# RWKV-7 time mixing on one core: each pair of heads with its r and v projections, low-rank products and chain together, beside a key projection of the next token group

## The chip, the core and the metric

The kernel runs on one NeuronCore of a Trainium2 chip. Its time is the device time of one launch in microseconds (us); the lower, the better. The engines are TensorE (PE, with its weight loads as PEld), VectorE (DVE), ScalarE (ACT), GpSimd (POOL) and SyncE (SP, which here issues nearly all DMAs). Each takes its instructions in a fixed order and waits on semaphores for what the others produce.

## The reference

One inference step of a two-layer hybrid decoder with D = 1024, on 1048 tokens: 16 learned tokens and 1024 prompt tokens in one sequence, and 8 decode tokens with states of their own. Layer 0 is a causal Conformer convolution, layer 1 is RWKV-7 time mixing with 16 heads of 64; after each comes a squared-ReLU MLP (1024 to 4096 to 1024). Layer 1 is what the change touches:

```python
xr, xw, xk, xv, xa, xg = (h + xx * x_mix[i] for i in range(6))   # xx = previous row - h
r, k, v = xr @ w_r, xk @ w_k, xv @ w_v
w_log = -softplus(-(w0 + tanh(xw @ w1) @ w2)) - 0.5
decay = exp(-exp(w_log))
a = sigmoid(a0 + (xa @ a1) @ a2)
g = sigmoid(xg @ g1) @ g2
kk = normalised per head (k * k_k)
k = k * (1 + (a - 1) * k_a)
S = S * decay + (S @ -kk) (kk * a) + v k      # step by step over the tokens, per head
y = S @ r
out = ((groupnorm(y) + bonus(r, k, v)) * g) @ w_o
```

## The kernel before

Everything lies feature by token: a tile has 128 features (one pair of heads, index p of 8) on the partitions and the tokens along the row. Layer 0 and its MLP run first and end at 1126 us of the trace. Then comes time mixing, which the change rewrites, then the output projection `w_o` and the second MLP.

**Token groups.** Time mixing takes the 1048 tokens in four groups `G1` of 272, 256, 256 and 264 (g = 0 to 3). For each, `prepare(g)` (line 773) loads the normalised rows `hx` and makes the differences `xx`; `mix` (line 808) makes one mixed input tile `mx` on DVE. `mixer_in(g)` (line 822) then has three stretches:

- eight r projections (lines 927 to 940; `proj`, line 848, is eight 128x128 weight blocks against eight `mx` tiles, 16 records in the trace), each copied out by ACT and written to DRAM (`d_rk`); then the narrow product for the gate (`narrow`, line 867, `p_g`), which reads `hx` directly;
- eight k projections (lines 951 to 966), written to `d_rk` too, each with the second gate product (`lora2`, `l_g`) and with its squares summed over heads by a matmul into `pn`; then the norms (`r16`) and the narrow product for decay and a (`p_wa`);
- eight v projections (lines 1043 to 1102), one for each pair of heads. With them goes the **chain** of that pair: `l_w` and `l_a` (second low-rank products), the spread of the norms (`pb`, line 1063), then on DVE and ACT the normalised key, the running sum of the log decay, two exponentials and the four scaled operands `ab` (lines 1064 to 1096), then in `finish` (line 984), one pair later, transposes of v (`vt`), small matmuls of 64 rows by 32 columns (`nn`, line 1015), the bonus (`pk`, line 1031), and DMAs to `d_ab`, `d_v`, `d_n` and `d_bv`. r and k come back from `d_rk` by `fetch` (line 1037).

**The recurrence.** Tokens are also cut into 17 chunks of up to 64 (`chunk`, line 1202). Chunk c needs the `ab` of all eight pairs of its group, and so runs beside the next group. Its `front` (line 1150) loads the operands, makes the products `A` and, once for four chunks, on DVE the `inverses` (line 1124) of 32x32 blocks (`tt`, `ni`: 60 instructions in a row that each need the one before). Then come the small matmuls `gg`, `po`, `W`, `U`, `S`, `Y` with DVE and ACT steps between them, which must follow one another. How far the recurrence goes beside the projections is set by `tick` (line 1420): each call adds `PACE[g]` to a credit, and chunks advance as far as the credit pays (`advance`, line 1318). In the v stretch `beside` gives half as much for a call (`VSLOW`) and steps `prepare` of the next group. What is left of the recurrence runs beside `w_o` and the MLP of the first output group (`until`), as do the decode tokens (`decode_step`) and the normalisation and gating of y (`norm_gate`).

**What sets the order.** The code states the dependences and a priority; the tile framework puts every engine's instructions into a fixed order when the kernel is built. Weight blocks (512 KB) go through `load_raw` (line 143) into a ring of six buffers, four projections ahead.

Of the kernel before, what the change touches and what calls it, by code (L numbers as in the profile page):

```python
# [8 lines left out]
F32 = mybir.dt.float32  # L9
# [3 lines left out]
ALU = mybir.AluOpType  # L13
# [35 lines left out]
def hybrid_step(tc, x_prompt, x_sample, state_conv, state_shift, state_wkv, meta_tokens,  # L49
# [10 lines left out]
    with ctx:  # L60
        def pool(stack, name, bufs, **kw):
            return stack.enter_context(tc.tile_pool(name=name, bufs=bufs, reuse_waits="tile", **kw))
# [14 lines left out]
        d_rk = dram.tile([P, KT, 2, T], F32, name="d_rk")  # L77
# [113 lines left out]
        def bank(name, tag="mm"):  # L191
            return cur[tag].tile([P, 512], F32, name=name, tag=tag)
# [577 lines left out]
        prep = {}  # L770
        VSLOW = 0.5

        def prepare(g):
# [34 lines left out]
            def mix(i, k):  # L808
# [8 lines left out]
        wrkv = col_stream([(w, p, f"w{s}{g}_{p}") for g in range(4)  # L817
                           for s, w in (("r", rwkv_w_r[0]), ("k", rwkv_w_k[0]), ("v", rwkv_w_v[0]))
                           for p in range(KT)], 4)
        carry = {"tail": lambda: None}  # L820

        def mixer_in(g, tick, ahead):
# [22 lines left out]
            def mixed(i):  # L845
                return [mix(i, k) for k in range(KT)]

            def proj(w, act, wid, name, fill=None):
                ps = bank(nm("p", name))
                for k in range(KT):  # L850
                    nc.tensor.matmul(ps[:wid, :n], w[:, k, :], act[k], start=k == 0, stop=k == KT - 1)  # L851
                    if fill and k in (2, 5):
                        fill()
                return ps
# [50 lines left out]
            def second(parts, name):  # L905

                raw = wide.tile([P, D], F32, name=nm(name) + "_raw", tag="wide")
                for rows, src in parts:
                    nc.sync.dma_start(raw[rows], src)
                return blocks_of(raw)  # L910

            dd = lambda p, i, src: nc.gpsimd.tensor_copy(ddec[:, p, i, :], src)
            allp = slice(0, P)

            def beside(gen, places, slow=1.0):

                calls = [0]

                def trace():
                    tick(slow)  # L920
                    if calls[0] % 3 in places:
                        next(gen, None)
                    calls[0] += 1
                return trace


            act = mixed(0)
            both = lambda: tick(1.0)
            for p in range(KT):
                both()  # L930
                ps = proj(next(wrkv), act, P, f"r{p}", both)
                if p == 0:
                    carry["tail"]()
                if p == KT - 2:
                    ws = narrow_w(1, "g")
                r = t_("st", p, "em", 2)
                nc.scalar.copy(r[:, :n], ps[:, :n])
                nc.sync.dma_start(d_rk[:, p, 1, c0:c0 + n], r[:, :n])
                if npr < n:
                    dd(p, 4, r[:, npr:n])  # L940


            gate(ws)
            act = mixed(2)
            pn = bank(nm("pn"), "x")
            wg2 = second([(allp, rwkv_g2[0])], "wg2")
            add_pn = lambda: None

            def to_pn(p, sq):
                return lambda: nc.tensor.matmul(pn[:, :n], head_sel(p), sq[:, :n], start=p == 0, stop=p == KT - 1)  # L950
            for p in range(KT):
                both()
                ps = proj(next(wrkv), act, P, f"k{p}", both)
                k_ = t_("st", p + KT, "em", 2)
                nc.scalar.copy(k_[:, :n], ps[:, :n])
                nc.sync.dma_start(d_rk[:, p, 0, c0:c0 + n], k_[:, :n])
                sq = t_("sq", p, "rk", 2)
                nc.scalar.activation(sq[:, :n], ps[:, :n], AF.Square, scale=vec("k_k", p))
                add_pn()
                add_pn = to_pn(p, sq)  # L960
                if p == KT - 2:
                    ws = narrow_w(0, "wa")
                ps = lora2(wg2, p, lg, f"g{p}")
                gt = t_("gt", p, "vv", 2)
                nc.scalar.copy(gt[:, :n], ps[:, :n])
                nc.sync.dma_start(d_g[:, p, c0:c0 + n], gt[:, :n])
            r16 = lorap.tile([P, N1], F32, name=nm("r16"), tag="lf")
            r16p = [lorap.tile([P, N1], F32R, name=nm("r16" + q), tag="r16" + q)[:, :n] for q in "hl"]

            def norms():  # L970
                add_pn()
                nc.vector.tensor_scalar(r16[:, :n], pn[:, :n], L2_EPS * L2_EPS, None, op0=ALU.max)
                nc.scalar.activation(r16[:, :n], r16[:, :n], AF.Sqrt)
                nc.vector.reciprocal(r16[:, :n], r16[:, :n])
                split(*r16p, r16[:, :n], nc.vector)

            norms()
            decay_rate(ws)


            act = mixed(3)
            both = beside(ahead, (1, 2), VSLOW)
# [54 lines left out]
            def fetch(p):  # L1037
                rk2 = pr.tile([P, 3, N1], F32, name=nm("rk2", p), tag="rk2", bufs=2)
                nc.sync.dma_start(rk2[:, 1:, :n], d_rk[:, p, :, c0:c0 + n])
                return rk2  # L1040

            late, later = (lambda: lambda: None), lambda: None
            for p, rk2 in ahead_of(fetch):
                both()
                if p == 0:
                    ps = proj(next(wrkv), act, P, f"v{p}", both)
                    wa2 = second([(HALF[0], rwkv_w2[0]), (HALF[1], rwkv_a2[0])], "wa2")
# [7 lines left out]
                if p:  # L1055
                    ps = proj(next(wrkv), act, P, f"v{p}", both)
# [5 lines left out]
                pb = bank(nm("pb", p), "x")  # L1062
# [39 lines left out]
                next(ahead, None)  # L1102
            for _ in ahead:
                pass
# [313 lines left out]
        PACE = [0, 1.7, 1.7, 0.98]  # L1418

        def tick(g, slow):  # L1420

            advance(PACE[g] * slow, NCH - 1)
            next(ng0, None)

        for g in range(4):
            if g == 0:
                for _ in prepare(0):
                    pass
            mixer_in(g, lambda slow=1.0: tick(g, slow), ranked(PP, prepare(g + 1)) if g < 3 else iter(()))
# [162 lines left out]
```

## Time and profile before

| what | value |
|---|---|
| time, median of 3 runs | 2861.14 us (2853.25 to 2863.94) |
| profiled execution, its own time | 2865.08 us |
| its span | 2863.4 us, mean granted TensorE clock 0.975 |
| time mixing, first r projection to the last v projection's pair | 1126.5 to 1845 us |
| PE busy over the span | 2756.3 us (96%) |
| DVE, ACT, POOL busy | 1795.2, 1185.9, 1436.1 us |
| DMA traffic | 428.15 MB, mean 150 GB/s |

How to read it. Each engine's busy time is the union of its instructions' records. A busy PE can still be slow in two ways that the share does not show: the granted clock (column PEclk, 1.00 is full) and small matmuls that follow one another more slowly than they could. In a row of the timeline the first number is the start, the second the length of the merged records; as matmuls overlap, the cost of a row is the distance from its start to the next row's start. "idle before" names what the engine waited for last.

### The profile page before, as it was taken

Reading aid. Unit: us, or ns where it says so; the run is one execution under the profiler, and the core shown is the slowest. Engines: PE = TensorE matmul, PEld = TensorE weight load, DVE = VectorE, ACT = ScalarE, POOL = GpSimd, SP = SyncE. Lnnn points to the kernel's source line nnn. Section 1 sums busy time; section 2 is a strip of 40 time slices with the busy share of each in tenths; the row PEclk is TensorE's granted clock in tenths of the full one; section 3 lists DMA queues with packets and bytes.
Section 4 is the critical chain, followed back from the end, with each engine's and each line's share of the span. In section 5 each row is a group of like instructions: output and inputs, shape, how many; then the busy total and the mean of one; then the engine's idle time right before and its main releaser. Section 6 shows DMA issues by size and latency. Waiting matters only on the chain.

```text
span 2863.4 us, 51601 instructions
## 1 busy us (share of the span) xinstructions
PE 2756.3 (96%) x19594; PEld 2553.4 (89%) x19594; DVE 1795.2 (63%) x3618; ACT 1185.9 (41%) x2230; POOL 1436.1 (50%) x1983
## 2 busy tenths in 40 slices
PE   8999999999999899979999999979999999999998
PEld 7999999999999898858778877768889999999998
DVE  5999999995465545167455771679756764443444
ACT  5545444543364332232434643534345552222223
POOL 6677877987788774000000110265448783333332
PEclk9999999999999999989999999989999999999999
DMA  6663544454445643778768785675557742222211
GB/s 177 176 186 88 154 139 133 134 178 140 140 129 149 192 140 120 214 198 197 199 181 217 212 215 150 195 179 149 131 152 215 208 134 86 67 74 67 67 60 41
DMA packets 659270, 428.15 MB, mean 150 GB/s; under 512 B 126840, under 2 KB 609208, under 8 KB 659022
## 3 DMA queue, kind: packets, MB, share of 16 engines
q1 hardware_dynamic: 652780, 421.93, 52.1%
q10 hardware_dynamic: 6018, 2.89, 0.4%
q8 instruction: 155, 2.54, 0.4%
q14 instruction: 93, 0.76, 0.1%
q0 software_dynamic: 224, 0.03, 0.0%
HBM read 353.03 MB, written 72.66 MB: 149 GB/s over the span
## 4 chain that ended last, share of the span: by engine, by line
PE 37%; DVE 7%; POOL 5%; DMA 3%; issue 3%; ACT 1%; SPq 0%; DVEq 0%; POOLq 0%; ACTq 0%
PE ps_in L187 3%; PE ps_in L188 3%; PE ps_in L189 3%; POOL wo_lo L162 3%; PE out L187 3%; PE out L189 3%; PE out L188 3%; PE p_v L851 3%; PE p_k L851 2%; POOL wi_lo L162 2%; PE p_r L851 2%; PE A L1176 2%; DVE ni L1136 1%; DVE tt L1135 1%; PE U L1260 1%
## 5 line engine op out<-in xcount | busy, mean ns | idle before, releaser
L162 POOL TENSOR_TENSOR wo_lo<-wo_raw,wo_hi 128x256 fp32r<-128x256 f32 x736 | 563.4, 799 | 286.3 <-ACT wo_hi L157 267.4
L162 POOL TENSOR_TENSOR wi_lo<-wi_raw,wi_hi 128x256 fp32r<-128x256 f32 x640 | 490.5, 799 | 272.0 <-ACT wi_hi L157 259.7
L187 PE MATMUL out<-hh,wo_hi 128*128 128x352 f32 (+2 forms) x1536 | 502.7, 327 | 18.5 <-DVE h L340 9.3
L187 PE MATMUL ps_in<-m_h,wi_hi 128*128 128x352 f32 (+2 forms) x1536 | 498.8, 325 | 12.3 <-ACT m_h L269 11.5
L340 DVE TENSOR_TENSOR h<-h,out 128x352 f32<-128x352 f32 (+2 forms) x768 | 385.5, 509 | 188.3 <-PE out L189 187.2
L189 PE MATMUL out<-hl,wo_hi 128*128 128x352 f32 (+2 forms) x1536 | 494.8, 325 | 6.8 <-DVE hl L141 6.8
L188 PE MATMUL out<-hh,wo_lo 128*128 128x352 f32 (+2 forms) x1536 | 497.7, 324 | 0.0
L189 PE MATMUL ps_in<-m_l,wi_hi 128*128 128x352 f32 (+2 forms) x1536 | 497.0, 324 | 0.0
L188 PE MATMUL ps_in<-m_h,wi_lo 128*128 128x352 f32 (+2 forms) x1536 | 496.7, 324 | 0.0
L504 DVE SCALAR_TENSOR_TENSOR cv<-u,wdw,cv 128x352 f32<-128x352 f32 (+2 forms) x720 | 376.5, 572 | 0.7
L157 ACT CAST wi_hi<-wi_raw 128x1024 fp32r<-128x1024 f32 x160 | 168.0, 1050 | 396.5 <-PE out L189 189.0
L157 ACT CAST wo_hi<-wo_raw 128x1024 fp32r<-128x1024 f32 x184 | 192.8, 1049 | 311.5 <-PE out L189 144.1
L187 PEld LDWEIGHTS out<-hh,wo_hi 128*128 128x128 f32 x1536 | 292.2, 190 | 26.3 <-DVE h L340 13.7
L187 PEld LDWEIGHTS ps_in<-m_h,wi_hi 128*128 128x128 f32 x1536 | 290.9, 189 | 15.6 <-ACT m_h L269 11.7
L189 PEld LDWEIGHTS out<-hl,wo_hi 128*128 128x128 f32 x1536 | 291.7, 191 | 9.0 <-DVE hl L141 8.1
L188 PEld LDWEIGHTS out<-hh,wo_lo 128*128 128x128 f32 x1536 | 292.2, 190 | 1.3
L188 PEld LDWEIGHTS ps_in<-m_h,wi_lo 128*128 128x128 f32 x1536 | 290.7, 189 | 1.7
L189 PEld LDWEIGHTS ps_in<-m_l,wi_hi 128*128 128x128 f32 x1536 | 290.6, 189 | 1.8
L327 DVE SCALAR_TENSOR_TENSOR r<-ps_in,rs_m 128x352 f32<-128x352 f32 (+2 forms) x192 | 98.5, 515 | 235.7 <-PE ps_in L189 232.0
L141 DVE TENSOR_TENSOR hl<-s,hh 128x352 fp32r<-128x352 f32 (+2 forms) x192 | 143.8, 750 | 112.0 <-ACT hh L140 111.9
L329 ACT ACTIVATE s<-r 128x352 f32<-128x352 f32 (+2 forms) x192 | 93.7, 490 | 141.6 <-DVE r L327 141.3
L851 PE MATMUL p_r<-mx,wr_raw 128*128 128x256 f32 (+2 forms) x512 | 123.4, 396 | 4.1 <-DVE n L1017 4.1
(350 smaller groups left out, 4926.9 us busy)
## 6 DMA issues: line engine op xcount, KB each, us to landing
wi_raw<-in_w_mlp_in_dram SPq DMA_DIRECT2D x160, 512.0 KB, 4.0
wo_raw<-in_w_mlp_out_dram SPq DMA_DIRECT2D x160, 512.0 KB, 3.7
wr_raw<-in_rwkv_w_r_dram SPq DMA_DIRECT2D x32, 512.0 KB, 6.0
wk_raw<-in_rwkv_w_k_dram SPq DMA_DIRECT2D x32, 512.0 KB, 4.2
wv_raw<-in_rwkv_w_v_dram SPq DMA_DIRECT2D x32, 512.0 KB, 4.5
d_ab<-ab SPq DMA_DIRECT2D x32, 512.0 KB, 4.0
pg_raw<-in_conv_w_pw_dram SPq DMA_DIRECT2D x24, 512.0 KB, 4.6
pa_raw<-in_conv_w_pw_dram SPq DMA_DIRECT2D x24, 512.0 KB, 4.7
```

The source lines that it names most:

```text
L141: eng_lo.tensor_sub(lo, src, hi.bitcast(F32))
L157: nc.scalar.copy(hi[:, :a * b], raw[:, :a * b])
L162: eng_lo.tensor_sub(lo[:, cs], raw[:, cs], hi[:, cs].bitcast(F32))
L187: nc.tensor.matmul(ps, w[0], act[0], start=first, stop=False)
L188: nc.tensor.matmul(ps, w[1], act[0], start=False, stop=False)
L189: nc.tensor.matmul(ps, w[0], act[1], start=False, stop=last)
L327: nc.vector.scalar_tensor_tensor(r[:, :n], ps[:, :n], 0.0, rs[:, :n], op0=ALU.max, op1=ALU.mult)
L329: nc.scalar.activation(s[:, :n], r[:, :n], AF.Square)
L340: nc.vector.tensor_add(hv[:, 4 * i + m, :], hv[:, 4 * i + m, :], ps[:, :n])
L504: nc.vector.scalar_tensor_tensor(acc[m][:, :n], ug[:, m, j:j + n], wdw[:, m, j:j + 1], acc[m][:, :n], op0=ALU.mult, op1=ALU.add)
L851: nc.tensor.matmul(ps[:wid, :n], w[:, k, :], act[k], start=k == 0, stop=k == KT - 1)
L1176: nc.tensor.matmul(ps[:, i * 2 * P:(i + 1) * 2 * P], bk[:, j + i, :], xa[:, j + i].rearrange("p q x -> p (q x)"), start=True, stop=True)
```

## The change

- The order of time mixing. The key projections, with their squares, are taken out of `mixer_in` into a generator `keys(g)`. Those of group 0 run ahead of everything; those of group g+1 run one by one beside the pairs of group g. `mixer_in(g)` starts with both narrow products (gate, then decay and a), and then has one loop over the eight pairs: r projection, `l_g`, `l_w`, `l_a`, v projection, the chain, `finish` of the pair before, and one key projection of the next group.
- r no longer goes to DRAM and back: it is copied straight into the pair's tile `rk2`. `d_rk` (r and k) becomes `d_k`.
- `g2`, `w2`/`a2`, the second low-rank weights, are loaded once and kept, not once for each group.
- The gate's sigmoid is written with Tanh (0.5 tanh(x/2) + 0.5).
- Buffers: weight ring 6 to 5, narrow weights 4 to 2, mixed inputs 20 to 25; `st`, `gt` get tags of their own, and `r16h`/`r16l` two buffers.
- `pb` takes its PSUM bank from the common pool of four (`mm`) and no longer from the single one (`x`), which `pn` holds while the keys of a group are projected.
- `prepare(g + 1)` is stepped whole at the first pair, not spread over the v stretch. Every call of `tick` counts 1.0, with `PACE` of 2.0 in groups 1 to 3.

```diff
-        cur["raw"] = pool(ld, "wrawd", 6)
-        wide = pool(ld, "wided", 4)
-        mixp = pool(ld, "mixp", 20)
+        cur["raw"] = pool(ld, "wrawd", 5)
+        wide = pool(ld, "wided", 2)
+        mixp = pool(ld, "mixp", 25)
...
+        def blocks_used():
+            for p in range(KT):
+                yield "k", 0, p
+            for g in range(4):
+                for p in range(KT):
+                    yield "r", g, p
+                    yield "v", g, p
+                    if g < 3:
+                        for kp in keys_of(p):
+                            yield "k", g + 1, kp
+
+        def keys_of(p):
+            return [p - 1] * (p > 0) + [p] * (p == KT - 1)
...
+        def keys(g, fill):
+            c0, n = G1[g]
+            nm = lambda s, *a: f"{s}{g}" + "".join(f"_{x}" for x in a)
+            mix = prep[g][0]
+            act = [mix(2, k) for k in range(KT)]
+            pn = bank(nm("pn"), "x")
+            add_pn = lambda: None
...
+            for p in range(KT):
+                yield
+                ps = proj(next(wrkv), act, n, nm("k", p), fill)
+                k_ = pr.tile([P, N1], F32, name=nm("st", p), tag="st", bufs=2)
+                nc.scalar.copy(k_[:, :n], ps[:, :n])
+                nc.sync.dma_start(d_k[:, p, c0:c0 + n], k_[:, :n])
+                sq = pr.tile([P, N1], F32, name=nm("sq", p), tag="rk", bufs=2)
+                nc.scalar.activation(sq[:, :n], ps[:, :n], AF.Square, scale=vec("k_k", p))
+                add_pn()
+                add_pn = to_pn(p, sq)
...
+            add_pn()
+            nc.vector.tensor_scalar(r16[:, :n], pn[:, :n], L2_EPS * L2_EPS, None, op0=ALU.max)
+            nc.scalar.activation(r16[:, :n], r16[:, :n], AF.Sqrt)
+            nc.vector.reciprocal(r16[:, :n], r16[:, :n])
+            split(*r16p, r16[:, :n], nc.vector)
...
             def gate(ws):
                 ps = narrow(ws, "g")
-                nc.scalar.activation(lg[:, :n], ps, AF.Sigmoid)
+                nc.scalar.activation(lg[:, :n], ps, AF.Tanh, scale=0.5)
+                nc.scalar.activation(lg[:, :n], lg[:, :n], AF.Copy, scale=0.5, bias=0.5)
...
+            wg, ww = narrow_w(1, "g"), narrow_w(0, "wa")
             act = mixed(0)
...
+            gate(wg)
+            decay_rate(ww)
+            carry["tail"]()
+            act_v = mixed(3)
+            r16p = norm.pop(g)
+            ks = iter(())
...
             for p, rk2 in ahead_of(fetch):
                 both()
-                if p == 0:
-                    ps = proj(next(wrkv), act, P, f"v{p}", both)
-                    wa2 = second([(HALF[0], rwkv_w2[0]), (HALF[1], rwkv_a2[0])], "wa2")
+                ps = proj(next(wrkv), act, n, nm("r", p), both)
+                nc.scalar.copy(rk2[:, 2, :n], ps[:, :n])
...
+                ps = lora2(wg2, p, lg, f"g{p}")
+                gt = t_("gt", p, "gt", 2)
+                nc.scalar.copy(gt[:, :n], ps[:, :n])
+                nc.sync.dma_start(d_g[:, p, c0:c0 + n], gt[:, :n])
...
-                if p:
-                    ps = proj(next(wrkv), act, P, f"v{p}", both)
+                ps = proj(next(wrkv), act_v, n, nm("v", p), both)
...
-                pb = bank(nm("pb", p), "x")
+                pb = bank(nm("pb", p))
...
                 late = finish(p, rk, ab, vv)
-                next(ahead, None)
-            for _ in ahead:
-                pass
+                if g < 3:
+                    if p == 0:
+                        for _ in ranked(PP, prepare(g + 1)):
+                            pass
+                        ks = keys(g + 1, both)
+                        next(ks)
+                    for _ in keys_of(p):
+                        next(ks, None)
...
-        PACE = [0, 1.7, 1.7, 0.98]
+        PACE = [0, 2.0, 2.0, 2.0]
...
+                for _ in keys(0, lambda: None):
+                    pass
+            mixer_in(g, lambda slow=1.0: tick(g, slow))
```

More of the change, by code (lines that the diff above doesn't have):

```diff
@@ L768, in hybrid_step, with second @@
             nc.scalar.copy(t[HALF[1 - i]], hsel[HALF[1 - i], 0:1].broadcast_to([HS, N1]))
-        prep = {}
-        VSLOW = 0.5
+        def second(parts, name):
+            raw = lorap.tile([P, D], F32, name=name)
+            for rows, src in parts:
+                nc.sync.dma_start(raw[rows], src)
+            return blocks_of(raw)
+        wg2 = second([(slice(0, P), rwkv_g2[0])], "wg2")
+        wa2 = second([(HALF[0], rwkv_w2[0]), (HALF[1], rwkv_a2[0])], "wa2")
+        prep, norm = {}, {}
         def prepare(g):
@@ new lines, in keys_of, with proj @@
+        def keys_of(p):
+            return [p - 1] * (p > 0) + [p] * (p == KT - 1)
+        w_of = {"r": rwkv_w_r[0], "k": rwkv_w_k[0], "v": rwkv_w_v[0]}
+        wrkv = col_stream([(w_of[s], p, f"w{s}{g}_{p}") for s, g, p in blocks_used()], 4)
+        def proj(w, act, n, name, fill=None):
+            ps = bank(f"p{name}")
+            for k in range(KT):
+                nc.tensor.matmul(ps[:, :n], w[:, k, :], act[k], start=k == 0, stop=k == KT - 1)
+                if fill and k in (2, 5):
+                    fill()
+            return ps
@@ L927, in mixer_in @@
-            act = mixed(0)
[L928 to L931, printed above, removed]
-                if p == 0:
[L933 to L940, printed above, removed]
@@ L943, in mixer_in @@
[L943 to L966, printed above, removed]
@@ L977, in mixer_in @@
[L977 to L982, printed above, removed]
+            dd = lambda p, i, src: nc.gpsimd.tensor_copy(ddec[:, p, i, :], src)
+            both = lambda: tick(1.0)
+            wg, ww = narrow_w(1, "g"), narrow_w(0, "wa")
+            act = mixed(0)
+            gate(wg)
[4 more added lines that the diff above has]
+            ks = iter(())
             def finish(p, rk, ab, vv):
```

46 lines of the change are left out of this document (9 added, 37 removed).

## The prediction

> **What bounds the kernel now.** I read the page's head first, then the busy time of each engine stretch by stretch, then who waits for whom in the worst stretch, then the timeline of PE.
>
> ```profile
> span 2863.4 us, 51601 instructions
> PE 2756.3 (96%) x19594; PEld 2553.4 (89%) x19594; DVE 1795.2 (63%) x3618; ACT 1185.9 (41%) x2230; POOL 1436.1 (50%) x1983
> ```
>
> PE is busy for 96% of the span, so time can only come from PE's idle time, from a lower granted clock, or from matmuls that follow one another slowly. The table has time mixing cut at the borders of its stretches (r and k, then v, for groups 0 to 3), then the `w_o` stage, then the MLP beside which the recurrence ends.
>
> ```profile
> core 0: us, PE busy (x) PEld busy (x) DVE busy (x) ACT busy (x) POOL busy (x), PEclk, DMA share, GB/s
> 1126.50:1207.80 81.30, 81.30 (x355) 67.19 (x354) 10.24 (x15) 16.52 (x38) 4.00 (x12) 1.00 0.73 216
> 1207.80:1280.10 72.30, 56.06 (x464) 42.80 (x463) 48.50 (x118) 32.98 (x104) 6.11 (x21) 0.89 0.70 201
> 1280.10:1388.10 108.00, 103.57 (x737) 86.90 (x738) 59.08 (x176) 29.55 (x81) 4.54 (x8) 0.96 0.81 198
> 1388.10:1476.20 88.10, 86.21 (x782) 64.66 (x780) 54.22 (x119) 41.35 (x111) 8.73 (x18) 0.92 0.68 184
> 1476.20:1584.10 107.90, 107.90 (x893) 89.59 (x893) 54.06 (x127) 43.25 (x99) 6.56 (x10) 0.99 0.83 219
> 1584.10:1667.00 82.90, 80.27 (x994) 63.76 (x994) 61.64 (x143) 53.24 (x145) 9.18 (x21) 1.00 0.81 208
> 1667.00:1784.70 117.70, 115.83 (x919) 91.65 (x918) 46.90 (x124) 35.85 (x86) 9.07 (x18) 1.00 0.69 182
> 1784.70:1845.00 60.30, 60.30 (x600) 47.52 (x598) 38.08 (x77) 32.72 (x100) 15.05 (x48) 1.00 0.53 152
> 1845.00:1930.00 85.00, 67.30 (x655) 59.12 (x654) 57.05 (x112) 39.04 (x75) 50.61 (x62) 0.82 0.78 203
> 1930.00:2290.00 360.00, 354.12 (x3019) 316.27 (x3018) 261.82 (x537) 166.25 (x316) 222.33 (x274) 0.97 0.62 170
> ```
>
> For each row I take as lost: the length less PE busy, and the length times what is missing in the clock (this counts an idle moment at a low clock twice, so it is an upper end). Row by row in time mixing: 0; 16.2 + 8.0; 4.4 + 4.3; 1.9 + 7.0; 0 + 1.1; 2.6; 1.9; 0: together **47 us**, of which 24 lie in the v stretch of group 0. There the recurrence has no chunk yet, and PE has only the v projections to put beside the chains. Who it waits for:
>
> ```profile
> PE pb L740 <- DVE rk L1064: 6.6, 2, 5.6
> PE p_r L851 <- DVE n L1017: 4.1, 1, 4.1
> 1235.06 0.49 PE L740 MATMUL pb<-r16h,hspread 128*128 128x272 f32 x1
> 1240.52 0.45 PE L1015 MATMUL nn<-ab 64*32 64x32 f32 x32
> ```
>
> From a pair's `pb` to its `nn` PE has 1240.52 - 1235.06 = 5.5 us of other work. In these the DVE steps of the chain must run:
>
> ```profile
> L1064 DVE SCALAR_TENSOR_TENSOR rk<-rk,negs,pb 128x256 f32<-128x256 f32 (+2 forms) x32 | 15.4, 481 | 33.5 <-PE pb L740 20.8 <-DMA rk<-d_rk 8.2 <-PE p_v L851 4.4
> L1083 DVE TENSOR_TENSOR wa<-rk,wa 128x512 f32<-128x512 f32 (+2 forms) x32 | 22.3, 696 | 1.6 <-ACT wa L1080 0.9
> L1086 DVE SCALAR_TENSOR_TENSOR rk<-rk,pvec,wa 128x256 f32<-128x256 f32 (+2 forms) x32 | 15.5, 484 | 0.3
> L1095 DVE TENSOR_TENSOR ab<-rk,ex 128x512 f32<-128x512 f32 (+1 forms) x40 | 24.5, 629 | 6.0 <-ACT ex L1071 5.4 <-issue 0.2
> L1096 DVE TENSOR_TENSOR ab<-wa,em 128x512 f32<-128x512 f32 (+1 forms) x40 | 23.4, 602 | 0.0
> ```
>
> 0.48 + 0.70 + 0.48 + 0.63 + 0.60 = 2.9 us, with the running sum, a second `ab` in group 0 and `mx` tiles of the next group between them. So 5.5 us is too little whenever DVE has anything else in its queue.
>
> **The change, part by part.**
>
> *PE's work.* The built order of the changed kernel has the same matmuls in all. By the first `w_o` product it has finished twelve chunks and not ten; these two move from the MLP into time mixing. Net zero.
>
> *The pairs.* A projection of 272 columns and a small product beside it cost:
>
> ```profile
> 1167.51 0.62 PE L892 MATMUL l_g<-lg,wg_raw 128*128 128x272 f32 x2
> 1167.96 3.83 PE L851 MATMUL p_k<-mx,wk_raw 128*128 128x272 f32 x16
> 1171.63 0.62 PE L892 MATMUL l_g<-lg,wg_raw 128*128 128x272 f32 x2
> ```
>
> that is 3.67 and 0.45 us. In the changed order three projections and four such products (`l_g`, `l_w`, `l_a`, `pn`) stand between `pb` and `nn` of one pair: 11.0 + 1.8 = 12.8 us in place of 5.5. In group 3, without keys, two projections and three products: about 8.7. That covers a chain of 2.9 us of DVE even with as much again queued ahead, so the losses inside the v stretches go. What is late next is each group's first pair. `hx` and `ni` of the next group are loaded after `p_wa` and the last pair's `d_n`, on one SP queue, and DVE takes the first inverse before or just after the first `rk`:
>
> ```profile
> DVE tt L1135 <- DMA ni<-d_n: 20.5, 4, 7.5
> d_n<-n SPq DMA_DIRECT2D x32, 64.0 KB, 4.4
> g_raw<-d_lr SPq DMA_DIRECT2D x8, 512.0 KB, 3.2
> ```
>
> d_n lands after 4.4 us, ni (512 KB) after 3.2 or more (the row of the same size), then xx, eight mx and the chain, some 9 us: 17 to 20 us, against about 18 us of PE work from the last pair's `nn` to the next group's first (four projections of 3.67 x 256 / 272 = 3.45 us, seven products, `A`, `pb`, `vt`). It hangs on the edge. I take 3.5 us of idle time for each of three borders, with a lowered clock after it (next paragraph, 3.4 us), 5 us for group 0's first pair, and 7 for two more drops inside: 21 + 5 + 7 = 33 remain of 47. **Gain 14** (bounds: 42, if only the first pair is late, and a loss of 25, if each border takes the 7.5 us of the wait row twice over with a drop).
>
> *The clock.* These are two neighbouring stretches of group 1's v part:
>
> ```profile
> 1423.30:1428.10 4.80, 4.80 (x61) 3.67 (x60) 0.73 (x2) 0.62 (x2) 1.04 (x2) 1.00 0.89 238
> 1428.10:1434.90 6.80, 6.80 (x27) 4.76 (x24) 4.37 (x9) 2.90 (x8) 0.11 (x1) 0.50 0.55 133
> ```
>
> PE was busy throughout the first, on `nn`, `W` and `po`, and still the clock fell to half for 6.8 us, which costs 3.4. So here a few us of small matmuls are enough. The Trainium skill (TensorE: Matmul & The Clock Gate, What's actually happening) puts the drop down to an idle window of about 3.4 us; by that alone no border of 3.5 us would be safe and no drop would come inside a group, so the sum would gain 7 more. The row speaks against reading it so: there was no idle time ahead of this drop.
>
> *Fewer turns between kinds of matmul.* Small matmuls of different forms, taken in turn, cost more than in a row:
>
> ```profile
> 1408.67 0.46 PE L1015 MATMUL nn<-ab 64*32 64x32 f32 x32 [1.89 <-DVE ab L1096]
> 1409.06 0.70 PE L1031 MATMUL pk<-rk,hsum 128*128 128x256 f32 x2
> ...
> 1425.69 0.25 PE L1015 MATMUL nn<-ab 64*32 64x32 f32 x2
> 1425.87 0.24 PE L1214 MATMUL po<-p,gg 32*32 32x32 f32 x2
> 1426.04 0.24 PE L1015 MATMUL nn<-ab 64*32 64x32 f32 x2
> ...
> 1442.17 0.70 PE L1176 MATMUL A<-xa,bk 128*128 128x256 f32 x2
> 1442.80 0.32 PE L1260 MATMUL U<-w,p 64*64 64x64 f32 x2
> 1443.06 0.70 PE L1176 MATMUL A<-xa,bk 128*128 128x256 f32 x2
> 1457.98 1.13 PE L1176 MATMUL A<-xa,bk 128*128 128x256 f32 x4
> 1459.04 0.57 PE L1276 MATMUL Y<-sv,xa 128*64 128x64 f32 x12
> ```
>
> 32 `nn` in a row take 1409.06 - 1408.67 = 0.39 us, 0.024 for two; in turn with `po` two take 0.17 to 0.18: 0.15 for each turn. With large ones, `A` takes 0.63 for two in turn and 1.06 / 2 = 0.53 in a row: 0.10, and `U` 0.26, so 0.1 to 0.2 a turn. I counted the turns in both built orders from the first projection to the first `w_o` product: small after another small 118 before and 66 after, between small and large 348 and 270: 130 fewer, at 0.14 us 18 us. Some fall where PE would wait anyway; I take three quarters, **14 us** (bounds 0 and 18).
>
> *Loads, buffers, tables.* 32 writes of r and nine loads of second low-rank weights go from SP, and the Sigmoid's table loads from ACT (they stand beside `p_g` and `p_wa` on PE); DMA runs at 0.53 to 0.83 of its time in mixing, and ACT at about half, so I count nothing. Against that, two narrow buffers in place of four let `wa_raw` be loaded only once half of `p_g` is done: the 3.2 us of the `g_raw` row behind 3.5 us of `p_g`, hidden but for SP's queue; with that cover gone 3.2 us in four groups, 13 us. The ring of five instead of six still loads four projections ahead. Taken: 0 (bounds: 3 gained, 13 lost).
>
> *After mixing.* Two chunks fewer beside the MLP relieve PE, already counted, and DVE, which is busy 57 of 85 us in the `w_o` row and 262 of 360 in the next. But in the changed order the last inverses stand ahead of the fourth `z_l` tile and no longer behind the sixth. **Gain 2** (bounds: 10 either way).
>
> Sum: 14 + 14 + 0 + 2 = 30. The profiled execution took 2865.08 us (1.7 around its span): 2835. It stands 3.9 us above the median of 2861.14; from that, **2831**.
>
> **The rivals.**
>
> *The borders eat it (about no change).* The first pair of each group waits for xx and ni, with all DVE work behind that wait: the recurrence's `w`, `uv` and `sv` too. At 12 us of idle time and 3.4 of clock for each of three borders in place of 6.9, 25 of the 30 us go: 2856. For: the wait row above, four times, up to 7.5 us, and everything on one SP queue. Against: before, the same loads came late and the rows from 1476 on lose under 3 us each.
>
> *Clock drops in every pair (slower).* The chunks' small matmuls now go beside all pairs of groups 1 to 3, 24 in all, next to each pair's `nn`. If each pair has one drop like that at 1428.10, that is 24 x 3.4 = 82 us in place of the 5 drops (17 us) in my sum: 2831 + 65 = 2896. It decides against the change from 5 + 30 / 3.4 = 14 drops on. The Trainium skill (TensorE: Matmul & The Clock Gate, A second HAM failure mode) tells of a kernel that idled briefly between groups of matmuls often enough for its clock to swing so. For: the drop came with PE busy. Against: the v stretch of group 2 holds eight pairs and much of the recurrence at a clock of 1.00, and each pair now has two or three large blocks where it had one.
>
> *All of it comes.* Only the first pair is late, turns cost as counted: 42 + 18 + 10 = 70 us: 2791.
>
> **How the numbers follow.** A measurement of this kernel can tell about 0.5% (14 us) from no change. My forecast, with gains from 15 to 61 us: 0.62. All of it: 0.06. The borders: 0.20. Clock drops: 0.12. So faster 0.68, the same 0.20, slower 0.12. The forecast and the borders' case, with 2866 as the end of the latter, give a range of 2800 to 2868; beyond it lie the clock drops and what is below 2800.
>
> **What would show it.** In the changed profile, group 0's pairs at a PE share near 1.00 and clock 1.00; the time from first projection to first `w_o` product about 8 us shorter although two more chunks (some 22 us of PE) are in it; DVE waits for `ni` and `xx` as the largest left, once in each group; fewer records of two `nn` or `po` between others. I am wrong if the clock column falls below 0.95 inside groups 1 to 3, if PE waits for `n` or `ab` in most pairs, or if the `w_o` stage grows beyond 85 us by what mixing saved.

## The result: 30 us slower, and the profile after

The changed kernel takes 2891.82 us (median of 4 runs, 2885.56 to 2896.42), the kernel before 2861.44 us in the same comparison (2853.25 to 2863.94): a ratio of 1.011, with a 95% interval of 1.0082 to 1.0138. The prediction was 2831 us, faster. The profiled execution of the changed kernel took 2896.42 us. The head of its page:

```profile
span 2894.7 us, 51574 instructions
PE 2781.4 (96%) x19594; PEld 2573.7 (89%) x19594; DVE 1785.7 (62%) x3618; ACT 1187.1 (41%) x2233; POOL 1436.8 (50%) x1983
```

The same 19594 matmul records as before keep PE busy for 25 us longer; DVE and ACT do no more than before. Where the 25 us lie can be seen when both traces are cut at the same three events: the first projection of time mixing, the first `w_o` product, and the first `w_o` product of the second output group. What lies between the second and the third is called **the stage** from here on: `w_o` and the MLP of the first output group, beside which the recurrence ends. The windows of the kernel before (length, then PE and the other engines, the granted clock, DMA):

```profile
1126.60:1858.40 731.80, 704.74 (x5923) 564.68 (x5922) 376.19 (x902) 293.31 (x778) 66.20 (x159) 0.97 0.74 198
1858.40:2282.40 424.00, 400.43 (x3435) 357.19 (x3434) 311.16 (x633) 194.49 (x369) 266.77 (x328) 0.95 0.63 173
```

and of the changed kernel:

```profile
1124.20:1855.60 731.40, 693.05 (x6356) 569.72 (x6354) 387.86 (x938) 311.73 (x821) 80.67 (x178) 0.97 0.72 189
1855.60:2313.70 458.10, 439.78 (x3002) 374.62 (x3001) 294.77 (x594) 177.56 (x329) 253.23 (x310) 0.91 0.54 150
```

The reader is to see three things. Time mixing, which was rewritten, takes as long as before, with 433 more records in it (two chunks' worth). The part after the stage takes 581.0 us in both. And the stage, whose code the change does not touch, is 34 us longer **although it holds 433 records fewer**: PE is busy for 96% of it, at a lower clock (0.91 for 0.95). The one long wait of PE in it, 12.1 us for `m_h`, stands in the kernel before too (11.5 us); PE itself is slow. The timeline of PE in the changed kernel shows how:

```profile
2050.65 0.33 PE L1268 MATMUL Y<-sv,xa 128*64 128x64 f32 x2
2050.91 0.41 PE L187 MATMUL ps_in<-m_h,wi_hi 128*128 128x328 f32 x1
2051.25 0.33 PE L1268 MATMUL Y<-sv,xa 128*64 128x64 f32 x2
2051.51 0.41 PE L188 MATMUL ps_in<-m_h,wi_lo 128*128 128x328 f32 x1
```

One small matmul of the recurrence (`Y`, two records) and one large one of the MLP (`ps_in`) take turns: 2051.25 - 2050.65 = 0.60 us a step. A form is small when its weight block is smaller than 128x128. One **turn** is a place in PE's order where a small form follows another form or is followed by one, so this step has two. I counted the turns in the built orders, as the prediction did, but now in the stage too: 255 before, **475 after**. Counted in the traces, by the weight blocks of the records, they are 275 and 506, close to what was built.

### The profile page after: what moved, and what is told of

Its sections match the earlier page's. It is cut to its first block, busy times and chain, and to the rows that moved or that the text cites. A ratio compares the mean times of both kernels' runs of the same rounds, so it can differ in the third digit from the quotient of the medians.

```text
span 2894.7 us, 51574 instructions
## 1 busy us (share of the span) xinstructions
PE 2781.4 (96%) x19594; PEld 2573.7 (89%) x19594; DVE 1785.7 (62%) x3618; ACT 1187.1 (41%) x2233; POOL 1436.8 (50%) x1983
## 4 chain that ended last, share of the span: by engine, by line
PE 75%; DVE 9%; POOL 6%; DMA 4%; issue 3%; ACT 2%; SPq 0%; DVEq 0%; ACTq 0%; POOLq 0%
PE out L187 7%; PE out L189 7%; PE out L188 7%; PE ps_in L187 7%; PE ps_in L189 7%; PE ps_in L188 7%; PE pk L845 4%; POOL wo_lo L162 3%; PE pr L845 3%; PE pv L845 3%; POOL wi_lo L162 2%; PE A L1168 2%; DVE cv L504 1%; PE U L1252 1%; PE ps_g L187 1%
## 5 line engine op out<-in xcount | busy, mean ns | idle before, releaser
L187 PE MATMUL ps_in<-m_h,wi_hi 128*128 128x352 f32 (+2 forms) x1536 | 502.4, 327 | 12.7 <-ACT m_h L269 12.1
L845 PE MATMUL pv<-mx,wv_raw 128*128 128x256 f32 (+2 forms) x512 | 124.9, 398 | 5.5 <-ACT rk L1029 5.5
```

Source lines behind the costliest of these rows:

```text
L187: nc.tensor.matmul(ps, w[0], act[0], start=first, stop=False)
L845: nc.tensor.matmul(ps[:, :n], w[:, k, :], act[k], start=k == 0, stop=k == KT - 1)
```

## The experiments

The theory: a turn costs about 0.2 us of PE (an estimate; the prediction's rows gave 0.1 to 0.2), and the changed kernel has 220 more of them in the stage, because what is left of the recurrence is handed out there more thinly. `until` spreads the remaining chunks over a share of the MLP's points that is fixed by FA (1.57); with two chunks fewer left, each point gets fewer of their steps, and the built order then mixes them one by one with the MLP's matmuls. The rivals: the rewritten mixing costs the time; the clock alone; DVE and ACT set the end of the stage.

The table holds what the experiments and both kernels showed: turns counted in the built orders (in mixing, in the stage), chunks whose `S` records lie in the stage (the expectations use the code's own count, six before and four after), and the lengths of mixing and stage, cut as above.

| kernel | turns, mixing | turns, stage | chunks left | mixing us | stage us | median us |
|---|---|---|---|---|---|---|
| before | 466 | 255 | 7 | 731.8 | 424.0 | 2861.44 |
| after | 336 | 475 | 5 | 731.4 | 458.1 | 2891.82 |
| e1, after, recurrence first in the stage | 337 | 76 | 5 | 719.9 | 374.9 | 2810.25 |
| e2, before, the same | 451 | 98 | 5 | 754.7 | 375.1 | 2835.39 |
| e3, after, FA 3.2 | 336 | 100 | 5 | 724.2 | 374.1 | 2813.92 |
| e4, after, FA 1.2 | 336 | 579 | 5 | 724.1 | 483.8 | 2920.45 |
| e6, before, first everywhere | 328 | 71 | 4 | 768.2 | 371.3 | 2847.13 |
| e7, after, first everywhere | 347 | 71 | 5 | 738.5 | 374.8 | 2819.63 |
| e8, as e1, PACE 1.7 | 736 | 110 | 6 | 801.9 | 385.0 | 2898.04 |
| e9, after, FA 2.36 | 336 | 173 | 5 | 734.0 | 401.8 | 2844.09 |
| e10, before, PACE 1.8 in group 3 | 550 | 415 | 4 | 772.6 | 469.0 | 2950.83 |
| e11, after, old PACE | 703 | 282 | 8 | 779.4 | 430.1 | 2921.65 |
| e12, as e1, PACE 2.3 | 318 | 81 | 5 | 724.8 | 369.6 | 2814.19 |

The lengths are of one profiled execution each. Mixing in the same order (after, e3, e4, e9) came out between 724.1 and 734.0, and e1, which has one turn more in it, at 719.9; so a difference of under 15 us in that column says little.

### e1 to e4: the turns in the stage

**e1**, the changed kernel with one number altered, the rank that `until` gives the recurrence's instructions:

```diff
-        RE = 0
+        RE = 4000
```

> The changed kernel with one number altered: the recurrence's instructions beside the MLP get a higher rank in the scheduler (RE = 4000 for 0). In its built order the w_o stage and the MLP's first group hold 76 turns between a small and another kind of matmul where the changed kernel has 475, with the same matmuls; mixing has the same order but for one turn. Theory (turns between small and large matmuls made the stage beside the end of the recurrence grow by 34 us): that stage, 458 us from first w_o product to the second group's, falls by 399 turns at 0.15 to 0.25 us, 60 to 100 us, less what PE then waits for the chain of chunks; 2800 to 2850 in all. Rival A (mixing itself is what costs, turns are hidden): within 10 us of 2892. Rival B (only the granted clock: small matmuls pull it down however they lie): 2880 to 2900. Rival C (DVE and ACT set the stage's end): more waits of PE, 2892 or more.

2810.25 us, 0.9816 of the kernel before (0.9786 to 0.9845): 82 us less than the changed kernel, and less than the kernel before. With mixing in the same order but for one turn, the rewritten mixing can't have been the loss. DVE, ACT and POOL do the same work in a stage of 375 us (DVE 297 us in e1, 295 in the changed kernel), so they did not set its end at 458. The small matmuls now lie in a row:

```profile
2088.54 0.99 PE L1261 MATMUL S<-uv,bkt 128*64 128x64 f32 x28
...
2090.29 1.10 PE L1271 MATMUL Y<-uv,nr 128*64 128x64 f32 x30
2091.32 0.41 PE L189 MATMUL ps_in<-m_l,wi_hi 128*128 128x328 f32 x1
```

30 `Y` records in 2091.32 - 2090.29 = 1.03 us, 0.07 for two, where a step with one `ps_in` took 0.60 above. The groups by line and form over the whole stage, first of the changed kernel, then of e1 (count, then busy time):

```profile
L1271 PE MATMUL Y<-uv,nr 128*64 128x64 f32 x160 | 21.3, 245 | 0.0
L1268 PE MATMUL Y<-sv,xa 128*64 128x64 f32 x160 | 19.0, 255 | 0.0
L1261 PE MATMUL S<-uv,bkt 128*64 128x64 f32 x160 | 15.2, 240 | 0.8 <-DVE uv L1253 0.8
L1206 PE MATMUL po<-p,gg 32*32 32x32 f32 x160 | 11.1, 210 | 0.0
```

```profile
L1268 PE MATMUL Y<-sv,xa 128*64 128x64 f32 x160 | 8.3, 245 | 2.0 <-DVE nr L1176 2.0
L1261 PE MATMUL S<-uv,bkt 128*64 128x64 f32 x160 | 7.4, 243 | 2.0 <-DVE uv L1253 1.9
L1271 PE MATMUL Y<-uv,nr 128*64 128x64 f32 x160 | 7.1, 230 | 0.0
L1206 PE MATMUL po<-p,gg 32*32 32x32 f32 x160 | 3.5, 192 | 0.0
```

The same 640 records: 66.6 us in turns, 26.3 in rows. The mean length of one (245 and 230 ns) hardly tells the two apart; the group's busy time (the union of its own records) does.

**e2**, the same number in the kernel before:

> The kernel before with the same altered rank (RE = 4000): 98 turns in the w_o stage and the MLP's first group where it has 255; in mixing 451 where it has 466. Theory of turns: 157 fewer at 0.15 to 0.25 us, 24 to 39 us less, so 2822 to 2838. If the mixing rewrite and not the turns made the changed kernel slower: no change from 2861 here.

2835.39 us, 0.9907 (0.9871 to 0.9943), within what the theory expected. The kernel before paid for its turns too. This edit did one thing more than the expectation says: two chunks moved from the stage into mixing (7 to 5 left), which became 23 us longer while the stage became 49 us shorter.

**e3** and **e4** leave the rank as it was and alter only how densely the rest is handed out:

```diff
-            NGA, NGB, FA, FB = 262.15, 45.48, 1.57, 40
+            NGA, NGB, FA, FB = 262.15, 45.48, 3.2, 40      # e3; 1.2 in e4
```

> The changed kernel with FA = 3.2 for 1.57: the same rank, but the recurrence's last chunks are handed out twice as densely, at the beginning of the MLP's points; 100 turns in the stage for 475. Theory of turns: like the first run, 2800 to 2850. If the altered rank did something else in the first run (a shorter chain, other buffers), this one stays near 2892.

> The changed kernel with FA = 1.2 for 1.57: the last chunks handed out more thinly; 579 turns in the stage for 475. Theory of turns: 104 more at 0.15 to 0.25 us, 16 to 26 us slower than the changed kernel, 2907 to 2918. Rival (a crowd of small matmuls, not turns, costs): a thinner spread is faster, under 2880.

e3: 2813.92 us, 0.9819 (0.9779 to 0.9859). e4: 2920.45 us, 1.02 (1.0167 to 1.0234), 2 us above the expected range. So it is not the rank as such: another way to fewer turns gives the same time, and a way to more of them costs more. The stage goes with its turns: from e1 over the changed kernel to e4, 374.9, 458.1 and 483.8 us at 76, 475 and 579 turns, 0.21 us for each turn (83.2 / 399) and 0.25 (25.7 / 104). The windows row of e4's stage:

```profile
1851.40:2335.20 483.80, 461.90 (x3003) 383.43 (x3002) 297.53 (x595) 176.65 (x330) 250.68 (x310) 0.91 0.52 142
```

3003 records keep PE busy for 461.90 us; in the changed kernel 3002 take 439.78. DVE, ACT and POOL are as busy as there, to within 3 us.

### e5: the price of a turn by itself

A kernel that only runs matmuls on loaded data, in an order written by hand:

```diff
+        for f in (Y, U, G, A, F):      # 128x64, 64x64, 32x32, 128x128 on 256 and on 64 columns
+            many(48, L, f)             # 48 large ones (L), then 48 steps of f
+            turns(48, L, f)            # the same, one by one
+        many(48, U, G)
+        turns(48, U, G)
+        many(48, Y, U)
+        turns(48, Y, U)
+        turns(24, L, Y, Y)
+        turns(12, L, Y, Y, Y, Y)
```

> No part of the reference is computed: only rows of matmuls of the kernel's forms on loaded data, first in a row, then in turn one by one, in a written order. Large: 128x128 weights, 328 columns (as ps_in). Small, two to a step: 128x64 on 64 columns (as Y and W), 64x64 (as U), 32x32 (as gg, po and nn); for comparison 128x128 float32 on 256 columns (as A) and on 64. Theory of turns: a step of large and two small takes 0.3 to 0.5 us more in turn than the sum of its parts in a row (two turns at 0.15 to 0.25 us), with nothing to wait for and the clock at 1.00; small forms in turn with one another 0.1 to 0.2 us a turn. Rival (the slow alternation of the changed kernel comes from waits on other engines or from the clock): in turn as in a row to within 0.05 us.

The timeline of PE, `L` with the 128x64 form (two records each, two to a step):

```profile
30.20 5.11 PE L85 MATMUL tiny<-small 128*64 128x64 f32 x166
35.24 0.42 PE L73 MATMUL big<-hi 128*128 128x328 f32 x1
35.59 0.34 PE L85 MATMUL tiny<-small 128*64 128x64 f32 x4
...
64.68 7.42 PE L73 MATMUL big<-hi 128*128 128x328 f32 x48
72.03 5.82 PE L89 MATMUL tiny<-small 64*64 64x64 f32 x192
```

In a row: `L` (72.03 - 64.68) / 48 = 0.153 us, a small record (35.24 - 30.20) / 166 = 0.030, together 0.153 + 4 x 0.030 = 0.274 a step. In turn the 48 steps took (64.68 - 35.24) / 48 = 0.613. The step has two turns: (0.613 - 0.274) / 2 = **0.17 us a turn**. The price goes by the turn and not by the small record: `L` with two and with four steps of `Y` between takes 0.73 and 0.96 us, 0.34 and 0.33 more than the parts in a row. With a full 128x128 block on only 64 columns in place of the small form:

```profile
219.69 10.82 PE L81 MATMUL tiny<-small 128*128 128x64 f32 x96
230.32 0.40 PE L73 MATMUL big<-hi 128*128 128x328 f32 x1
230.56 0.33 PE L81 MATMUL tiny<-small 128*128 128x64 f32 x2
230.70 0.40 PE L73 MATMUL big<-hi 128*128 128x328 f32 x1
```

In a row 0.153 + 2 x (230.32 - 219.69) / 96 = 0.374, in turn 230.70 - 230.32 = 0.38: nothing. (`L` with `A`'s form gave nothing either: 0.580 a step for 0.581.) So it is not the short row of columns, nor the change of data or of operand type, but the **shape of the weight block** (with the place of the output that goes with it; the two weren't separated): here turns cost between a 128x128 block and a smaller one. Two different small shapes cost it too:

```profile
296.11 5.81 PE L89 MATMUL tiny<-small 64*64 64x64 f32 x192
301.86 0.34 PE L85 MATMUL tiny<-small 128*64 128x64 f32 x4
302.12 0.33 PE L89 MATMUL tiny<-small 64*64 64x64 f32 x4
302.38 0.34 PE L85 MATMUL tiny<-small 128*64 128x64 f32 x4
```

0.52 a step for 8 x 0.030 = 0.24: 0.14 a turn. In this kernel there is nothing to wait for, so a turn has its price without any wait on another engine. The Trainium skill (TensorEngine Tiling (Array Packing), Tiling Modes: Key Properties) says that to change the tiling mode, and not merely the tile, drains TensorE, without a price; these rows agree with it and give the price. By that rule the turns of the stage could have been looked for before the run.

The windows of the same kernel show what the clock does: the 128x64 turns, then two of the 32x32 turns, then 32x32 in a row (its last 0.7 us are turns with 64x64).

```profile
36.00:64.00 28.00, 28.00 (x230) 17.50 (x230) 0.00 (x0) 0.00 (x0) 0.00 (x0) 1.00 0.00 1
118.30:125.00 6.70, 6.70 (x56) 4.00 (x55) 0.00 (x0) 0.00 (x0) 0.00 (x0) 0.77 0.00 0
125.00:135.00 10.00, 10.00 (x61) 5.82 (x61) 0.00 (x0) 0.00 (x0) 0.00 (x0) 0.50 0.01 2
254.80:258.10 3.30, 3.30 (x174) 3.04 (x168) 0.00 (x0) 0.00 (x0) 0.00 (x0) 1.00 0.02 5
```

By its records PE is busy in all four (the ends of the records are modelled, so shorter pauses inside a turn wouldn't show). With 32x32 blocks in turn with large ones the clock falls to half and stays there as long as the turns last; with 128x64 it stays at full speed for 28 us. Whether 32x32 in a row would keep the clock is not shown: the longest row lasted 3.3 us, and the drop behind it came at 258.4, only 1.0 us after the turns with 64x64 had begun (257.4) and 4.3 us after the row had (254.1). A similar drop is to be seen in the changed kernel's stage, where `gg` (32x32) begins to take turns, and the windows around it:

```profile
2063.98 0.24 PE L1206 MATMUL gg<-x,no 32*32 32x32 f32 x2
2064.15 0.33 PE L1271 MATMUL Y<-uv,nr 128*64 128x64 f32 x2
2064.41 0.24 PE L1206 MATMUL gg<-x,no 32*32 32x32 f32 x2
```

```profile
2063.00:2067.60 4.60, 4.60 (x36) 3.20 (x35) 1.49 (x2) 1.89 (x3) 3.14 (x5) 1.00 0.17 26
2067.60:2081.30 13.70, 13.70 (x56) 10.19 (x55) 0.34 (x1) 3.43 (x7) 0.48 (x1) 0.50 0.31 77
```

There are drops of another kind too. The rows show a stretch of the changed kernel's stage before and during a drop, first beside turns of `pfs` (64x64) with `ps_in`, then after the wait for `m_h`:

```profile
2176.90:2183.70 6.80, 6.80 (x39) 4.33 (x37) 1.46 (x3) 2.78 (x8) 2.78 (x4) 1.00 0.60 142
2183.70:2193.90 10.20, 10.20 (x36) 8.08 (x36) 1.20 (x3) 3.01 (x5) 2.32 (x4) 0.50 0.35 94
1903.80:1910.60 6.80, 1.96 (x10) 1.39 (x8) 6.80 (x15) 1.07 (x3) 6.80 (x8) 1.00 0.42 145
1910.60:1920.80 10.20, 2.99 (x11) 2.99 (x12) 10.20 (x25) 4.35 (x10) 5.11 (x8) 0.50 0.46 129
```

In all, the clock of this stage is at 0.50 in nine stretches, 82 us. Six of them (61 us) follow turns with PE busy throughout, five with 32x32 blocks and one with 64x64, though 64x64 in turn with large ones kept 1.00 for 29 us in e5 (from 78 to 107); so the shape alone doesn't decide. Three (21 us) follow idle time. In e1 the clock is at 0.50 for 27 us in four stretches, all with 1.4 us or more of idle time in the 6.8 us before. So what the changed kernel lost in clock over e1 follows its turns; a further part, 21 and 27 us at half clock, follows waits in both.

In sum: the stage of the changed kernel keeps PE busy for 439.8 us and that of e1 for 338.9, 100.9 apart. By estimate, 399 turns at 0.17 are 68, and the clock takes 9% of 458.1 us against 4% of 374.9, 41 - 15 = 26. Together 94 of 100.9. Of the 101 the length shows 83, because in e1 PE waits for 36 us in the stage, in the changed kernel for 18.

### e6 to e8: what the work by pairs is worth

**e6** and **e7** give the recurrence the higher rank in mixing too, in the kernel before and in the changed one:

```diff
-        RC = 0
+        RC = 4000
...
-        RE = 0
+        RE = 4000
```

> The kernel before with the recurrence ranked first in mixing as well as beside the MLP (RC = RE = 4000): 328 turns in mixing for 466, 71 for 255 after it, about as many as the changed kernel with the same ranks has (347 and 71). Theory of turns at 0.17 to 0.2 us: 322 fewer, 55 to 64 us less than 2862, about 2800, and then the work by pairs itself is worth nothing beside the turns. If the pairs and the chain's shorter waits are worth the 14 us of the prediction: 10 to 20 us slower than the next run.

> The changed kernel with the recurrence ranked first in mixing too (RC = RE = 4000): 347 turns in mixing for 336, 71 after it. By turns as the first run, 2805 to 2815. It stands beside the run before this one: the same ranks, about the same turns, and the pairs as the difference.

2847.13 us (0.9926, 0.9902 to 0.995) and 2819.63 (0.9839, 0.9812 to 0.9866). The theory of turns alone missed here: e6, expected at about 2800, has 123 turns fewer in mixing than e2 and is 12 us slower; e7 came 5 us above its range and 9 above e1. The windows of mixing, e2 first and then e6:

```profile
1120.40:1875.10 754.70, 722.35 (x6244) 580.79 (x6243) 387.90 (x933) 307.47 (x810) 87.02 (x183) 0.95 0.75 199
```

```profile
1126.80:1895.00 768.20, 713.92 (x6564) 582.61 (x6562) 402.35 (x962) 314.17 (x832) 75.39 (x170) 0.96 0.74 194
```

PE's idle time goes from 32 to 54 us, so what the turns give is paid back in waits. That chunks pressed together have too little beside them in the old order is my reading of it; part of the longer mixing is one chunk more in it (320 records). With the pairs, e1 and then e7:

```profile
1130.60:1850.50 719.90, 688.29 (x6345) 566.26 (x6343) 386.60 (x935) 311.43 (x820) 79.41 (x176) 0.99 0.74 191
```

```profile
1128.90:1867.40 738.50, 702.82 (x6452) 575.00 (x6450) 391.94 (x939) 314.77 (x827) 83.44 (x180) 0.97 0.73 187
```

At the same ranks the changed kernel is faster than the kernel before by 25 us (e2 to e1) and by 27.5 us (e6 to e7, with 19 turns *more* in mixing): the work by pairs, with the turns that it saves, is worth that much, and the changed kernel's loss does not come from it.

**e8** is e1 with a slower handing out in mixing:

```diff
-        PACE = [0, 2.0, 2.0, 2.0]
+        PACE = [0, 1.7, 1.7, 1.7]
```

> The changed kernel with the rank of the first run (RE = 4000) and a slower handing out of the recurrence in mixing, PACE 1.7 for 2.0: the same matmuls, about two chunks fewer in mixing, but 736 turns there for 337, and 110 after it for 76. Theory of turns: 433 more at 0.15 to 0.25 us, 65 to 108 us slower than the first run, 2875 to 2918, and most of that in mixing. If turns between projections and small matmuls cost nothing there (PE waits for the chain anyway): 2810 to 2820.

2898.04 us (1.0111, 1.008 to 1.0142), as the theory of turns has it: mixing takes 82 us more than in e1 with one chunk fewer in it and 399 turns more.

### e9 to e12: pacing undone, and pacing alone

> The changed kernel with FA = 2.36 for 1.57, so that its four chunks left are handed out beside the MLP as densely as the six of the kernel before (4 x 2.36 = 6 x 1.57); the scheduler's ranks are as in both kernels. 173 turns in the w_o stage and the MLP's first group, where the changed kernel has 475 and the kernel before 255. Theory (the pacing of the rest, by its turns, is the whole loss of the changed kernel): that stage 375 + 97 x 0.21 = 395 us, 2825 to 2838 in all. If the ranks of the first run did the work and not the turns: near 2892.

2844.09 us (0.9917, 0.9893 to 0.9942), 6 us above the expected range. The edit is FA = 2.36 for 1.57 and nothing else. The stage takes 401.8 us for the 395 expected, and mixing fell out long in this profile (734.0 us).

With the old density of handing out, and the old ranks, the change is a gain of 24 us (with 173 turns in the stage, though, not the 255 of the kernel before).

**e10** makes the kernel before do what the changed one does to its rest, without the pairs:

```diff
-        PACE = [0, 1.7, 1.7, 0.98]
+        PACE = [0, 1.7, 1.7, 1.8]
```

> The kernel before with PACE of the last group 1.8 for 0.98: two chunks more are done in mixing, four are left for the MLP as in the changed kernel, and nothing of the work by pairs. 415 turns beside the MLP for 255, 550 in mixing for 466. Theory of turns at 0.17 to 0.21 us: 41 to 51 us slower than the kernel before, 2900 to 2915, with the stage beside the MLP 5 to 20 us longer though it holds two chunks fewer. If the loss of the changed kernel comes from the work by pairs: 2861, unchanged.

2950.83 us (1.0291, 1.0269 to 1.0313): the right way, but 36 us above the expected range, since the stage lost more than its turns at 0.21 us say. PE is idle in it for 41 us, against 24 in the kernel before, and of its 102 us at half clock 48 follow idle time, against 24. So a part of this loss is waits and not turns. Its clock is the lowest of all:

```profile
1899.80:2368.80 469.00, 428.35 (x2810) 363.72 (x2810) 295.05 (x590) 176.75 (x324) 251.16 (x314) 0.89 0.55 151
```

**e11** gives the changed kernel the old PACE back (the reverse of the last line of the diff above):

> The changed kernel with the old PACE (1.7, 1.7, 0.98 for groups 1 to 3): the work by pairs alone. Ten chunks are done before the w_o stage, as before; 282 turns after it for the 255 of the kernel before, but 703 in mixing for 466, since the chunks' steps are handed out more thinly between projections. Theory of turns at 0.2 to 0.26 us in mixing, less the 30 us that the pairs gain at equal turns: mixing 750 to 785 us, the stage beside the MLP about 430, 2885 to 2925 in all. If the pace had nothing to do with it: 2835 to 2860.

2921.65 us (1.019, 1.0167 to 1.0214), in the range of the theory of turns. So PACE 2.0 was not simply a mistake of the change: at the old pace the stage is about as before (430.1 us), and the turns lie in mixing instead, 703 of them. What fails is either pace together with the rank and the FA that were left alone.

> The changed kernel with the rank of the first run (RE = 4000) and PACE 2.3 for 2.0: 318 turns in mixing for 337, 81 after it for 76. Theory of turns: as the first run to within 5 us, 2803 to 2815. If what counts is how early the chunks are done: 2795 or less.

2814.19 us (0.9811, 0.9784 to 0.9838): no different from e1 and e3. These three versions beat both kernels, the kernel before by 52 to 56 us in the same comparisons; among the three the runs decide nothing. If how early the chunks are done had counted, e12 would have taken 2795 us or less.

## Why the prediction was wrong, point by point

**The step that failed: "After mixing ... Gain 2 (bounds: 10 either way)", together with the count of turns "from the first projection to the first `w_o` product".** The prediction had the mechanism and its price (0.14 us a turn, from rows between 1408 and 1459; e5 measured 0.14 to 0.17) and stopped counting at the border of the code that was changed. What it gave for the stage comes to 424 us less 22 for two chunks less 2, that is 400. It measured 458: by estimate 220 turns more at 0.17 us, 37 us, and 20 us of lower clock (41 us lost for 21), most of it beside turns. Those 58 us are nearly the whole miss of 61.

**Mixing, "14 + 14".** Right in sum, wrong in its parts, so in part by luck. Forecast were 28 us less, 22 of them filled with two chunks (an estimate): about 726 us. The four profiles of the same order gave 724.1 to 734.0, mean 728. But PE's idle time did not fall: it was 731.8 - 704.7 = 27 us before and 731.4 - 693.1 = 38 after. The gain came in PE's busy time, 12 us less with 433 records more: by estimate fewer turns, 130 at 0.17 or 22 us where 14 were taken, while the clock hardly moved (0.97 before, 0.97 to 0.98 in the four). In these profiles the term of the waits has the wrong sign. The sign named for group 0, a PE share near 1.00 at a clock of 1.00, did not come either:

```profile
1170.30:1310.00 139.70, 130.02 (x811) 107.30 (x810) 52.91 (x125) 47.30 (x141) 6.04 (x21) 0.96 0.75 202
```

The lower bound of this term, "a loss of 25", comes to 20 from its own numbers (47 less three times 15 + 3.4, less 12); nothing rests on it. How the 25 to 27 us of the pairs divide between turns, waits and clock isn't settled: e1 and e2 differ in turns and clock and not in idle time, e6 and e7 in idle time and not in turns.

**Rival "the borders eat it".** Not seen. The longest waits of PE in mixing, and the one for the narrow weights (total, times, longest), are in the changed kernel:

```profile
PE A L1168 <- DMA bk<-d_ab: 7.2, 3, 5.7
PE pv L845 <- ACT rk L1029: 5.5, 1, 5.5
...
PE p_wa L922 <- DMA wa_raw<-d_lr: 2.5, 2, 1.3
```

None is a first pair that waits for `ni` or `xx` (12 us were its price). A border does have a wait, of another kind: the 5.7 us, at 1305.6, are the first chunk's wait for the operands of group 0.

**Rival "clock drops in every pair" (2896 us).** It came within 4 us of the measured time by another way: the clock in mixing is 0.97 before and after. That the number is near is luck. The drops that were added lie in the stage, mostly beside `gg` and `po` taken in turn, and not beside the pairs' `nn`. The reading of the row at 1428.10 was right: no idle time went ahead of the drop, and e5 shows such drops with PE busy throughout. The Trainium skill (TensorE: Matmul & The Clock Gate, What's actually happening) ties the drop to an idle window. The stretch from 1910.60 agrees with that, the one from 2183.70 and e5's from 125 to 135 do not; there the measurement decides.

**Rival "all of it comes" (2791 us).** Not seen. It needed most of the 47 us counted as lost in mixing, and PE's idle time there rose by 11 us.

**Loads, buffers, tables, "0".** The two late `wa_raw` loads cost 2.5 us at `p_wa`, inside the bounds. Buffers weren't tried singly.

**"If the `w_o` stage grows beyond 85 us by what mixing saved"** was the nearest of the signs named, but it looked at a window that ends at 1930, and the paragraph behind it at DVE's queue. Up to 1930 the stage is 3 us longer than before (74.4 for 71.6), after that 31 (383.7 for 352.4).

## What to carry to other kernels

Count turns between shapes of weight blocks over the whole program, not only where the code changed: a change that moves work from one stage to another alters the mixture in both. Small matmuls that fill another stage's time should be ranked or handed out so that they lie in rows (one number here, worth 82 us), as long as enough other work stands beside them: ranked first in mixing too, e6 and e7 came out slower than e2 and e1. Fewer of them, spread thin, can cost more than many. In a profile the sign is a PE that is busy for nearly all of a stage with fewer records in it than in the other kernel, and stretches at a lower clock with no idle time ahead of them.

## What the runs showed of the hardware that I had not expected

- In e5 a turn cost 0.14 to 0.17 us where the shape of the weight block changed (128x128 with 128x64, 128x64 with 64x64), and nothing where only columns or operand type changed (0.38 us in turn for 0.374 in a row).
- The granted clock fell to 0.50 with PE busy throughout where 32x32 blocks took turns with other shapes (window 125 to 135 of e5; 2067.6 to 2081.3 of the changed kernel), and once beside 64x64 (2183.7 to 2193.9), while 128x64 in turn with large ones kept 1.00 for 28 us in e5.
